# Meta tokens in front of the second block's input tiles, four panels in two pieces of 264 columns

## The chip, the cores and the metric

The kernel runs on one core of one Trainium2 chip. The metric is the device time of one execution in microseconds (us): 1583.48 us, the median of 3 runs (1582.49 to 1584.28).

## The reference

Two transformer blocks, one after the other, on 512 tokens of width 1024. The part that the change touches is the entry of the second block. It puts 16 learned meta tokens in front of the 512 tokens, normalises every token by its root mean square, and projects all of them by one wide weight matrix:

```python
h = jnp.concatenate([jnp.zeros((b, PAD, d)), meta, x], axis=1)
hn = rms_norm_2(h, attn_norm_g[l])
proj = hn @ w_in[l]
aq, ak, av, bq, bkv, iq, ik, iw, gates = jnp.split(proj, IN_SPLITS_2, axis=-1)
```

Only the keys and values need the meta tokens: `ak` and `av` (keys and values of the sliding-window attention, which has sinks), `bkv` (the latent keys and values of the sparse attention) and `ik` (the keys of the indexer that chooses, for each query, the 128 rows that the sparse attention may see). `ik` goes through a layer norm, `bkv` through a root-mean-square norm. Queries and gates are needed for the 512 tokens alone.

## The kernel before, in words

Activations lie transposed in SBUF: features on the partitions, tokens along the row, so that a token tile is 128 x 512. Every float32 factor is split into a high and a low part (`xh`, `xl` for an input, `wh`, `wl` for a weight), and a product is three matmuls: high by high, high by low, low by high (`mm3`, line 654). A weight "panel" is 128 x 1024, eight pieces (k = 0 to 7) of 128 x 128; `dense` (line 659) runs a panel as 8 x 3 matmuls of 512 columns into one PSUM tile (`psd`; `pso` for the panel `2ik`). SyncE's queue loads a panel as `wr`, ScalarE casts it to `wh`, and in the second block's attention GpSimd makes the difference `wl` for every panel of 1024 columns (elsewhere VectorE does some or all).

The first block ends with a feed-forward stage, `ffn1` (line 1574). Its last eight panels (`fb0_3` to `fb7_3`) finish the tokens x[0] to x[7]; for each, `x_steps` (line 1644) makes the next input pair `xh`, `xl` (x times a gain, not yet times the norm) and adds squares for two norms. From these come R1 (the final norm of the first block) and then Rt (`R`, the second block's norm). The norm factor R is multiplied in when a panel's result is taken out of PSUM, so the panels `2iq0`, `2iq1`, `2ik`, `2ak`, `2av`, `2aq0` can start before R is known; `2bkv` comes some 100 us later, after eight gate panels.

The meta tokens go beside this. `meta_prep` (line 1750), called at the start of the second block's attention, loads them as a 128 x 8 x 16 tile, multiplies by the gain, splits them (`mh`, `ml`), squares them, and gets their norm by eight tiny float32 matmuls into a column `rm` of 16 rows. In the four panels with `meta=True`, `dense` issues three more matmuls for each k, with the 16 meta columns as weights and the panel's piece as the moving side (128 columns; 68 in `2ik`), into a PSUM tile `pss`. That result lies the other way round (tokens on the partitions). For `2ak` and `2bkv`, `meta_cols` (line 1860) scales it on VectorE (`mT`), turns it on TensorE, and copies it to the front of a 528-column tile; for `2av` it is scaled and split as it lies; for `2ik` it goes into the fifth part of the layer norm's tile.

The order of the work. All engines run their instructions in program order, and the program order comes from a planner in the kernel. `charge` (line 344) gives each instruction a cost: a matmul that is not plain float32 costs 0.42e-3 us per column, but at least 0.107. A panel's matmuls are emitted as they come; everything else is a chain of steps (`chain`, line 392), and a step is emitted as soon as the planned time of TensorE has passed the step's planned start (`pick`, line 413: earliest start first, then priority, then age). A step with a transpose thereby gets a fixed place between two k's of some panel. The planner knows nothing of one engine holding up another's memory access.

After `2aq0` the stage of the indexer and of the sliding-window attention begins (scores, softmax, transposes; VectorE also picks the top 128 of each row in rounds of 8).

Buffers: tiles `u` (34 slots), `v` (10 in the second block's attention, 42 in both feed-forward stages, `nvf`), and PSUM tiles `psd` 3, `pss` 2, `pst` 2, `pso` 1.

Of the kernel before, what the change touches and what calls it, by code (L numbers as in the profile page):

```python
# [8 lines left out]
F32 = mybir.dt.float32  # L9
F32R = mybir.dt.float32r  # L10
BF16 = mybir.dt.bfloat16
AF = mybir.ActivationFunctionType
OP = mybir.AluOpType
# [4 lines left out]
P = 128  # L18
T = 512
# [4 lines left out]
TK = T + NMETA  # L24
NEG = -1e30
# [227 lines left out]
class Prog:  # L253
    nu, nv1, nv2, nvf, nk = 34, 25, 10, 42, 7
# [404 lines left out]
    def dense(self, name, X, nk, evac, M=P, sub=1, meta=False, steps=1, tag="d"):  # L659

        whl = None
        for j in range(sub):
            if whl is None:
                whl = self.w_get(name)
            wh, wl = whl
            ps = self.ps(tag, steps)
            pm = self.ps("s") if meta else None
            for k in range(nk):
                x = X[k] if not callable(X) else X(k)
                if len(x) > 2:  # L670
                    self.ensure(x[2])
                o = (j * nk + k) * M
                a, b = wh[:, o:o + M], wl[:, o:o + M]
                self.mm3(ps[0:M], a, b, x[0], x[1], k == 0, k == nk - 1)
                if meta:
                    self.mm3(pm[0:NMETA, 0:M], self.mh[:, k], self.ml[:, k], a, b, k == 0, k == nk - 1)
                yield
            if meta:
                evac(j, ps, pm)
            else:  # L680
                evac(j, ps)
# [163 lines left out]
    def v_tile(self, label, ps, put):  # L845

        nc = self.nc
        st = {}

        def s1():  # L850
            st["t"] = self.scaled(ps)

        def s2():
            pt = self.ps("t", 2)
            for b in range(4):
                nc.tensor.transpose(pt[:, P * b:P * b + P], st["t"][:, P * b:P * b + P], self.ident)
            st["pt"] = pt[:].rearrange("p (b c) -> p b c", b=4)

        def s3():
            st["v"] = [self.v(F32R, (P, 4, P), name="vt") for _ in range(2)]  # L860
            for hh, vt in enumerate(st["v"]):
                self.hi(vt[:, :, 0:64], st["pt"][:, :, 64 * hh:64 * hh + 64])

        def s4():
            for hh, vt in enumerate(st["v"]):
                self.lo(vt[:, :, 64:128], st["pt"][:, :, 64 * hh:64 * hh + 64], vt[:, :, 0:64])
            put(st["v"])
        self.chain(label, s1, s2, s3, s4, after=("R",))
# [507 lines left out]
    def block1_attention(self):  # L1376
        nc, tc = self.nc, self.tc
        mm = nc.tensor.matmul
        with ExitStack() as c1:
# [11 lines left out]
            v1 = self.apool.tile([8, 640], F32, name="v1")  # L1391
            va, v2 = (self.apool.tile([P, PTW], F32, name="row", tag="pt%d" % x, bufs=1) for x in range(2))
            oh = []
# [250 lines left out]
    def x_steps(self, X, m, src, g, sts, pool):  # L1644

        hi, lo = pool(F32R, name="xh"), pool(F32R, name="xl")
        X[m] = (hi, lo)
        a, b = self.xg((hi, lo), src, g)

        def sq():  # L1650
            for n, scale in sts:
                self.sq_chain(n, m, src, scale)
        return [a, b, sq]
# [39 lines left out]
    def block1(self):  # L1693
# [4 lines left out]
        with ExitStack() as c:  # L1698
# [13 lines left out]
            X2 = {}  # L1712
            gg = self.v(shape=(P, 8), name="gg")
# [5 lines left out]
            def norms():  # L1719

                N["R1"] = self.rkeep.tile([P, T], F32, name="R1", tag="R", bufs=2)
                N["R"] = self.rkeep.tile([P, T], F32, name="Rt", tag="R", bufs=2)
                self.norm("R1", 0, x2, lambda: N["R1"][:])
                self.norm("pb", 1, x2, None, evac=lambda ps: nc.scalar.copy(N["R"], ps))
                self.chain("Rt", s2, *self.rstd_steps(lambda: st["t"][:], T, D, out=lambda: N["R"][:]), s3,
                           after=("pb", "R1"))
# [9 lines left out]
            def resid(m):  # L1736
# [4 lines left out]
                                                [(0, None), (1, self.pv("g_final", m))], self.u), norms)  # L1741
# [5 lines left out]
            self.X = lambda k: (self.ensure(("x", k)), X2[k])[1]  # L1747


    def meta_prep(self):  # L1750

        nc = self.nc
        mt = self.v(shape=(P, 8, NMETA))
        nc.sync.dma_start(mt, self.I["metaT"])
        self.mh = self.mpool.tile([P, 8, NMETA], F32R, name="mh")
        self.ml = self.mpool.tile([P, 8, NMETA], F32R, name="ml")
        t = self.v(shape=(P, 8, NMETA))
        self.rm = self.mpool.tile([P, 1], F32, name="rm")
        st = {}

        def s0():
            nc.vector.tensor_tensor(t, mt, self.pv("g2", 0, 8).unsqueeze(2).to_broadcast([P, 8, NMETA]), op=OP.mult)

        def s0a():
            self.hi(self.mh[:], t[:])
            nc.scalar.activation(mt, mt, AF.Square)

        def s0b():
            self.lo(self.ml[:], t[:], self.mh[:])

        def s1():
            st["ps"] = ps = self.ps("t")
            for k in range(8):
                nc.tensor.matmul(ps[0:NMETA, 0:2], mt[:, k], self.ones[:, 0:2], start=(k == 0), stop=(k == 7))
        self.chain("meta", s0, s0a, s0b, s1,
                   *self.rstd_steps(lambda: st["ps"][0:NMETA, 0:1], 1, D, rows=NMETA,
                                    out=lambda: self.rm[0:NMETA], tmp=lambda: self.small([P, 1])), at=8.0)

    def mT(self):
        return self.mpool.tile([P, P], F32, name=self.nm("mT"), tag="mT", bufs=2)  # L1780

    def idx_k(self):
        def ev(j, ps, pm):
# [3 lines left out]
            def s1():  # L1787
                st["t"] = self.scaled(ps, rows=68)
                k = st["k"] = self.tmp()
                k3 = st["k3"] = k[:, 0:320].rearrange("p (b c) -> p b c", b=5)  # L1790
                nc.gpsimd.memset(k3[:, 4], 0.0)
                nc.vector.tensor_scalar_mul(k3[0:NMETA, 4], pm[0:NMETA, 0:64], self.rm[0:NMETA])

            def s2():
                pt = self.ps("t")
                for b in range(4):
                    nc.tensor.transpose(pt[:, 68 * b:68 * b + 68], st["t"][0:68, P * b:P * b + P],
                                        self.ident[0:68, 0:68])
                st["z"] = pt[:, 0:272].rearrange("p (b c) -> p b c", b=4)

            def s3():
                k3, z = st["k3"], st["z"]
                nc.vector.tensor_copy(k3[:, 0:4], z[:, :, 0:64])
                nc.vector.tensor_scalar_mul(self.iw, z[:, :, 64:68], 0.0625)
# [4 lines left out]
                q = self.tmp()  # L1809
                q3 = q[:, 0:320].rearrange("p (b c) -> p b c", b=5)  # L1810
# [29 lines left out]
        yield from self.dense("2ik", self.X, KD, ev, M=68, meta=True, tag="o")  # L1840
# [19 lines left out]
    def meta_cols(self, st, ps, pm):  # L1860

        nc = self.nc

        def s1():
            f = st["f"] = self.kk()
            nc.vector.tensor_mul(f[:, NMETA:TK], ps, self.R)
            t = st["mt"] = self.mT()
            nc.vector.tensor_scalar_mul(t[0:NMETA], pm[0:NMETA, 0:P], self.rm[0:NMETA])

        def s2():  # L1870
            pt = st["pt"] = self.ps("t")
            nc.tensor.transpose(pt[:, 0:NMETA], st["mt"][0:NMETA], self.ident[0:NMETA, 0:NMETA])

        def s3():
            nc.vector.tensor_copy(st["f"][:, 0:NMETA], st["pt"][:, 0:NMETA])
        return [s1, s2, s3]

    def a_k(self):
        def ev(j, ps, pm):
            st = {}  # L1880

            def s4():
                for g in range(2):
                    self.stack_k("ak", st["f"], 64 * g, self.ak)
            self.chain("ak", *self.meta_cols(st, ps, pm), s4, after=("R", "meta"))
        yield from self.dense("2ak", self.X, KD, ev, meta=True)

    def a_v(self):
        def ev(j, ps, pm):
            nc = self.nc  # L1890
            self.v_tile("av", ps, self.av.extend)

            def s1():
                t = self.mT()
                nc.vector.tensor_scalar_mul(t[0:NMETA], pm[0:NMETA, 0:P], self.rm[0:NMETA])
                src = t[0:NMETA].rearrange("p (g d) -> p g d", g=2)
                self.split((self.avm[0:NMETA, :, 0:64], self.avm[0:NMETA, :, 64:128]), src)
            self.chain("av", s1, after=("meta",))
        yield from self.dense("2av", self.X, KD, ev, meta=True)

    def b_kv(self):
        def ev(j, ps, pm):
# [33 lines left out]
            self.chain("bkv", *self.meta_cols(st, ps, pm), s4, s5,  # L1936
# [3 lines left out]
        yield from self.dense("2bkv", self.X, KD, ev, meta=True)  # L1940
# [352 lines left out]
    def block2_attention(self):  # L2293
        nc, tc = self.nc, self.tc
        with ExitStack() as c:
# [21 lines left out]
            self.meta_prep()  # L2317
# [272 lines left out]
```

## Time and profile before

| | |
|---|---|
| median of 3 runs | 1583.48 us |
| the profiled execution | 1585.77 us, of which its span (first to last instruction) is 1584.0 us |
| TensorE busy | 1529.1 us, 97% of the span |
| VectorE busy | 914.6 us, 58% |
| ScalarE busy | 774.5 us, 49% |
| GpSimd busy | 251.7 us, 16% |
| granted clock of TensorE, mean | 0.984 of full speed |

In the profile a tile is named without its buffer number: `psd<-xh,wh` is a matmul into a `psd` tile with `xh` moving and `wh` as weights. PE is TensorE, PEld its weight loads, DVE VectorE, ACT ScalarE, POOL GpSimd. A matmul's duration includes its latency, so what a matmul costs in a stream is read from the distance between starts. A float32 matmul is recorded twice. All instructions are recorded by one helper (line 241), so groups are told apart by tiles and not by lines. `mk` is the top-k mask, `qs` the split queries, `kk` a 528-column tile, `cst` the identity for transposes, `Rt` the second block's norm.

### The profile page before, as it was taken

The page shows a single profiled execution, that of the slowest core. Times are in us where ns is not written, and L with a number is a line of the kernel's source. Part 1 is how long each engine was busy: PE and PEld are TensorE (multiplying, and loading weights), DVE is VectorE, ACT ScalarE, POOL GpSimd, SP SyncE. Part 2 cuts the span into 40 slices and gives each one's busy share as a digit, 9 for nine tenths or more (in the row PEclk, how much of TensorE's full clock was granted, in tenths as well). Part 3 has the DMA queues.
Part 4 walks back from the last instruction along what each step waited for, and adds up shares of the span by engine and source line. Part 5 has one row for each costly group of instructions (what it writes and reads, how often), then busy time and mean ns, then how long its engine had stood idle before and what let it go on. Part 6 is the DMA issues. An engine that isn't in the chain of part 4 may idle for free.

```text
span 1584.0 us, 19921 instructions
## 1 busy us (share of the span) xinstructions
PE 1529.1 (97%) x7400; PEld 1254.1 (79%) x7400; DVE 914.6 (58%) x1781; ACT 774.5 (49%) x1468; POOL 251.7 (16%) x176
## 2 busy tenths in 40 slices
PE   7999999999999999999998899899899999999997
PEld 3788888878888888888876787678688888888887
DVE  5587677762654243454576999666566432446445
ACT  5676687985343231323443784577544222332333
POOL 3344211102210000000233133321142000000001
PEclk9999999999999999999999999999999999999999
DMA  4444421113423333233323222231042233333411
GB/s 154 131 134 135 120 67 54 60 54 96 157 86 101 94 94 106 93 93 98 102 89 99 67 77 86 63 119 34 28 146 93 94 95 104 94 91 111 134 50 54
DMA packets 50257, 148.82 MB, mean 94 GB/s; under 512 B 6620, under 2 KB 10332, under 8 KB 50160
## 3 DMA queue, kind: packets, MB, share of 16 engines
q1 hardware_dynamic: 44352, 138.63, 28.0%
q0 software_dynamic: 3360, 4.46, 1.4%
q10 hardware_dynamic: 2448, 4.46, 0.8%
q8 instruction: 58, 0.95, 0.2%
q14 instruction: 39, 0.32, 0.1%
HBM read 138.11 MB, written 4.41 MB: 90 GB/s over the span
## 4 chain that ended last, share of the span: by engine, by line
PE 88%; DVE 7%; ACT 2%; DMA 1%; issue 1%; SPq 0%; POOL 0%; DVEq 0%; ACTq 0%; POOLq 0%
PE psd L241 75%; PE pss L241 5%; PE pso L241 4%; PE pst L241 4%; DVE tmp L241 1%; DVE sct L241 1%; DVE sm L241 1%; DVE qs L241 1%; DMA x<-xT 1%; ACT tmp L241 1%; DVE pt L241 0%; DVE P L241 0%; SPq L241 0%; DMA cscr<-c 0%; DVE ol L241 0%
## 5 line engine op out<-in xcount | busy, mean ns | idle before, releaser
L241 PE MATMUL psd<-xh,wh 128*128 128x512 f32 (+1 forms) x1128 | 453.8, 402 | 8.5 <-ACT xh L241 8.5
L241 PE MATMUL psd<-xh,wl 128*128 128x512 f32 (+1 forms) x1128 | 443.6, 393 | 1.6 <-DVE wl L241 1.6
L241 PE MATMUL psd<-xl,wh 128*128 128x512 f32 (+1 forms) x1128 | 443.5, 393 | 0.3 <-DVE xl L241 0.2
L241 ACT CAST wh<-wr 128x1024 fp32r<-128x1024 f32 (+1 forms) x232 | 242.1, 1044 | 350.1 <-PE psd L241 195.0
L241 POOL TENSOR_TENSOR wl<-wr,wh 128x1024 fp32r<-128x1024 f32 x72 | 178.3, 2478 | 531.3 <-ACT wh L241 511.4
L241 PEld LDWEIGHTS psd<-xh,wh 128*128 128x128 f32 (+1 forms) x1128 | 213.5, 189 | 52.6 <-ACT xh L241 9.8
L241 DVE TENSOR_TENSOR wl<-wr,wh 128x1024 fp32r<-128x1024 f32 (+1 forms) x160 | 195.9, 1225 | 99.2 <-ACT wh L241 97.0
L241 PEld LDWEIGHTS psd<-xh,wl 128*128 128x128 f32 (+1 forms) x1128 | 212.9, 189 | 48.6 <-DVE wl L241 2.0
L241 PEld LDWEIGHTS psd<-xl,wh 128*128 128x128 f32 (+1 forms) x1128 | 213.4, 189 | 43.9 <-issue 2.4
L241 ACT ACTIVATE P<-P,sm 128x256 f32<-128x256 f32 (+7 forms) x319 | 165.8, 545 | 27.7 <-DVE sm L241 27.2
L241 POOL TENSOR_TENSOR sq<-sq,tmp 128x512 f32<-128x512 f32 (+1 forms) x32 | 39.5, 1242 | 737.3 <-ACT tmp L241 730.9
L241 PE MATMUL psd<-hh,wl 128*128 128x512 f32 x384 | 149.4, 389 | 0.0
L241 PE MATMUL psd<-hl,wh 128*128 128x512 f32 x384 | 149.4, 389 | 0.0
L241 PE MATMUL psd<-hh,wh 128*128 128x512 f32 x384 | 149.4, 389 | 0.0
L241 PEld LDWEIGHTS psd<-hh,wl 128*128 128x128 f32 x384 | 72.1, 188 | 15.0
L241 PEld LDWEIGHTS psd<-hl,wh 128*128 128x128 f32 x384 | 72.1, 188 | 15.0
L241 PEld LDWEIGHTS psd<-hh,wh 128*128 128x128 f32 x384 | 72.1, 188 | 15.0
L241 DVE TENSOR_TENSOR pt<-pst,pt 128x384 fp32r<-128x384 f32 (+3 forms) x144 | 69.3, 498 | 16.5 <-ACT pt L241 15.7
L241 ACT ACTIVATE tmp<-psd 128x512 f32<-128x512 f32 x32 | 19.1, 597 | 106.8 <-PE psd L241 106.7
L241 DVE TENSOR_TENSOR tmp<-tmp 128x512 f32<-128x512 f32 (+1 forms) x33 | 22.7, 686 | 83.4 <-ACT tmp L241 83.4
L241 ACT CAST pt<-pst 128x384 fp32r<-128x384 f32 (+3 forms) x144 | 58.4, 439 | 16.5 <-PE pst L241 15.2
L241 PE MATMUL pst<-cst,P 128*128 128x128 f32 (+1 forms) x416 | 63.1, 280 | 2.7 <-DVE pt L241 2.7
(368 smaller groups left out, 2276.8 us busy)
## 6 DMA issues: line engine op xcount, KB each, us to landing
wr<-wall SPq DMA_DIRECT2D x231, 512.0 KB, 3.5
wr<-wall SPq DMA_DIRECT2D x8, 384.0 KB, 3.6
kk<-v2scr SPq DMA_DIRECT2D x8, 264.0 KB, 4.5
x<-xT SPq DMA_DIRECT2D x8, 256.0 KB, 8.3
wb<-v1scr SPq DMA_DIRECT2D x8, 256.0 KB, 3.8
xr<-xT ACTq DMA_DIRECT2D x8, 256.0 KB, 4.4
xscr<-xr SPq DMA_DIRECT2D x8, 256.0 KB, 2.0
x<-xscr ACTq DMA_DIRECT2D x8, 256.0 KB, 4.8
```

The source lines that it names most:

```text
L241: return f(*a, **k)
```

## The change

The second block's input pairs become 128 x 528, with the 16 meta columns in front (gain multiplied in, split); the other panels read columns 16 to 527. `meta_prep` moves to the start of `ffn1`'s last eight panels: the load of the meta tokens, their gain, their squares and the eight matmuls for their norm (now with the 128 x 128 tile of ones as weights and 16 moving columns, so that the norm comes out along a row, on all partitions) are issued there, and the norm is written to the front of the 528-column `Rf`. A new chain `("xm", m)` for each of the eight input tiles casts 16 columns on ScalarE and makes the difference on GpSimd.

A new `dense_meta` replaces `dense(meta=True)` for `2ik`, `2ak`, `2av`, `2bkv`: for each k, six matmuls of 264 columns, into two PSUM tiles (one of the panel's own kind, one `pss`). `scaled_meta` takes the result out in two VectorE multiplies of 248 and 264 columns and one of 16, or two of 264. With that `2ak` and `2bkv` lose the scaling, the turn and the copy for meta; `2av` and `2ik` get a turn of 16 columns more.

Besides, `nvf` goes from 42 to 41 (a small tile `gg` leaves that pool), an 8 x 640 tile `v1` early in the first block becomes a slice of a larger one, and the layer norm of `ik` uses one temporary less.

```diff
-    nu, nv1, nv2, nvf, nk = 34, 25, 10, 42, 7
+    nu, nv1, nv2, nvf, nk = 34, 25, 10, 41, 7
...
-                if meta:
-                    self.mm3(pm[0:NMETA, 0:M], self.mh[:, k], self.ml[:, k], a, b, k == 0, k == nk - 1)
...
+    def dense_meta(self, name, evac, M=P, tag="d"):
+
+        wh, wl = self.w_get(name)
+        ps = self.ps(tag), self.ps("s")
+        for k in range(KD):
+            self.X(k)
+            xh, xl = self.XM[k]
+            a, b = wh[:, k * M:k * M + M], wl[:, k * M:k * M + M]
+            for n, (w, x) in enumerate(((a, xh), (a, xl), (b, xh))):
+                for e in range(2):
+                    self.mms(ps[e][0:M, 0:HT], w, x[:, HT * e:HT * e + HT], k == 0 and n == 0, k == KD - 1 and n == 2)
+            yield
+        evac(ps)
+
+    def scaled_meta(self, dst, ps, rows=P, M=NMETA):
+
+        nc = self.nc
+        R, w = self.Rf, HT - M
+        nc.vector.tensor_mul(dst[0:rows, 0:w], ps[0][0:rows, M:HT], R[0:rows, M:HT])
+        nc.vector.tensor_mul(dst[0:rows, w:w + HT], ps[1][0:rows, 0:HT], R[0:rows, HT:TK])
+        if M:
+            m = self.small([P, M])
+            nc.vector.tensor_mul(m[0:rows], ps[0][0:rows, 0:M], R[0:rows, 0:M])
+            return m
...
     def meta_prep(self, R):
...
+                nc.tensor.matmul(ps[:, 0:NMETA], self.ones, mt[:, k], start=(k == 0), stop=(k == 7))
+        self.chain("mt", s0, at=4.0)
+        self.chain("meta", s1, *self.rstd_steps(lambda: st["ps"][:, 0:NMETA], NMETA, D, out=lambda: R[:, 0:NMETA],
+                                                tmp=lambda: self.small([P, NMETA])), after=("mt",))
...
-    def meta_cols(self, st, ps, pm):
+    def meta_cols(self, st, ps):
...
         def s1():
-            f = st["f"] = self.kk()
-            nc.vector.tensor_mul(f[:, NMETA:TK], ps, self.R)
-            t = st["mt"] = self.mT()
-            nc.vector.tensor_scalar_mul(t[0:NMETA], pm[0:NMETA, 0:P], self.rm[0:NMETA])
-
-        def s2():
-            pt = st["pt"] = self.ps("t")
-            nc.tensor.transpose(pt[:, 0:NMETA], st["mt"][0:NMETA], self.ident[0:NMETA, 0:NMETA])
-
-        def s3():
-            nc.vector.tensor_copy(st["f"][:, 0:NMETA], st["pt"][:, 0:NMETA])
-        return [s1, s2, s3]
+            st["f"] = self.kk()
+            self.scaled_meta(st["f"], ps, M=0)
+        return [s1]
...
-            self.meta_prep()
```

## Rows read from the trace of the kernel before

**Rows 1.** The page's chain that ended last, by engine

```profile
PE 88%; DVE 7%; ACT 2%; DMA 1%; issue 1%; SPq 0%; POOL 0%; DVEq 0%; ACTq 0%; POOLq 0%
```

**Rows 2.** Waits of PE, 800 to 1170 us: us in total, times, longest

```profile
PE pst L241 <- DVE tmp L241: 8.7, 2, 5.3
PE pss L241 <- DVE sm L241: 6.1, 4, 3.9
PE pst L241 <- DVE kk L241: 2.4, 1, 2.4
```

**Rows 3.** Windows: length, busy PE, PEld, DVE, ACT, POOL; clock; DMA share; GB/s

```profile
840.00:860.00 20.00, 20.00 (x111) 15.36 (x109) 8.36 (x21) 5.13 (x10) 7.87 (x8) 0.91 0.52 128
...
880.00:900.00 20.00, 15.78 (x84) 13.73 (x85) 17.35 (x52) 12.96 (x38) 2.40 (x1) 0.83 0.28 84
...
1000.00:1020.00 20.00, 16.73 (x66) 13.72 (x67) 10.64 (x16) 10.00 (x15) 4.34 (x2) 0.83 0.09 27
```

**Rows 4.** Timeline of PE in 2ik and 2ak: start us, us, instruction

```profile
824.55 0.43 PE L241 MATMUL pso<-xh,wh 128*68 128x512 f32 x1
...
829.50 0.47 PE L241 MATMUL psd<-xh,wh 128*128 128x512 f32 x1
...
844.44 0.44 PE L241 MATMUL psd<-xh,wh 128*128 128x512 f32 x1
...
845.18 0.22 PE L241 MATMUL pss<-wh,mh 128*16 128x128 f32 x1
...
845.36 0.45 PE L241 MATMUL psd<-xh,wh 128*128 128x512 f32 x1
```

**Rows 5.** Timeline of PE: matmuls of 272 and of 256 columns

```profile
863.46 0.41 PE L241 MATMUL pss<-kk,qs 128*128 128x272 f32 x2
863.71 0.40 PE L241 MATMUL psd<-xh,wh 128*128 128x512 f32 x1
...
1540.15 0.28 PE L241 MATMUL psd<-hl,wk 128*128 128x256 f32 x1
...
1540.51 0.28 PE L241 MATMUL psd<-hl,wk 128*128 128x256 f32 x1
```

**Rows 6.** Groups by form, PEld: the weight loads of these 256-column matmuls (busy us, mean ns)

```profile
L241 PEld LDWEIGHTS psd<-hh,wk 128*128 128x128 f32 x192 | 30.1, 192 | 0.1
```

**Rows 7.** Timeline of PE at the meta norm in 2ik

```profile
822.38 0.20 PE L241 MATMUL pss<-wl,mh 128*16 128x68 f32 x1
823.08 0.20 PE L241 MATMUL pss<-wh,ml 128*16 128x68 f32 x1 [0.50 <-DVE ml L241]
...
823.69 0.45 PE L241 MATMUL pso<-xh,wh 128*68 128x512 f32 x1
```

**Rows 8.** Timeline of PEld, then of PE: a 16-column float32 matmul with the ones

```profile
975.28 0.19 PEld L241 LDWEIGHTS pst<-kk,ones 128*128 128x128 f32 x1 [0.24 <-issue]
...
975.42 0.48 PE L241 MATMUL psd<-xh,wh 128*128 128x512 f32 x1
```

**Rows 9.** Timeline and window (busy PE, clock) of PE around the long wait

```profile
837.77 0.71 PE L241 MATMUL pst<-cst,tmp 68*128 68x68 f32 x4 [5.29 <-DVE tmp L241]
...
838.23:843.39 5.16, 5.16 (x21) 0.50 0.75 242
```

**Rows 10.** Timeline of DVE from the norm to 2ik's scaling

```profile
818.67 2.48 DVE L241 TENSOR_TENSOR v<-v,pvt 128x128 f32<-128x128 f32 x1
...
829.50 1.27 DVE L241 SCALAR_TENSOR_TENSOR tmp<-psd,Rt 128x512 f32<-128x512 f32 x2
...
832.13 4.87 DVE L241 TENSOR_TENSOR qs<-tmp,qs 64x512 fp32r<-64x512 f32 x4
837.02 0.69 DVE L241 TENSOR_TENSOR tmp<-pso,Rt 68x512 f32<-68x512 f32 x1
```

**Rows 11.** Timeline of POOL in the same stretch

```profile
818.47 2.53 POOL L241 TENSOR_TENSOR wl<-wr,wh 128x1024 fp32r<-128x1024 f32 x1 [6.21 <-ACT wh L241]
...
833.91 2.54 POOL L241 TENSOR_TENSOR wl<-wr,wh 128x1024 fp32r<-128x1024 f32 x1 [5.87 <-ACT wh L241]
```

More of the change, by code (lines that the diff above doesn't have):

```diff
@@ L24 @@
 TK = T + NMETA
+HT = TK // 2
 NEG = -1e30
@@ L657, in mm3, with dense @@
         self.mms(ps, al, bh, False, stop)
-    def dense(self, name, X, nk, evac, M=P, sub=1, meta=False, steps=1, tag="d"):
+    def dense(self, name, X, nk, evac, M=P, sub=1, steps=1, tag="d"):
         whl = None
@@ L666, in dense @@
             ps = self.ps(tag, steps)
-            pm = self.ps("s") if meta else None
             for k in range(nk):
@@ L674, in dense @@
                 self.mm3(ps[0:M], a, b, x[0], x[1], k == 0, k == nk - 1)
-                if meta:
-                    self.mm3(pm[0:NMETA, 0:M], self.mh[:, k], self.ml[:, k], a, b, k == 0, k == nk - 1)
                 yield
[L678 to L681, printed above, removed]
+            evac(j, ps)
+    def dense_meta(self, name, evac, M=P, tag="d"):
[19 more added lines that the diff above has]
+            return m
     def rstd_steps(self, ps, w, n, rows=P, out=None, tmp=None):
@@ L843, in c_rows, with v_tile @@
         self.chain(label, lambda: self.dma(t[64:68], self.cscr[h, r:r + 4]), after=("fl",))
-    def v_tile(self, label, ps, put):
+    def v_tile(self, label, ps, put, meta=None):
         nc = self.nc
@@ L850, in s1 @@
         def s1():
-            st["t"] = self.scaled(ps)
+            if meta is None:
+                st["t"] = self.scaled(ps)
+            else:
+                st["t"] = self.tmp()
+                st["m"] = self.scaled_meta(st["t"], ps)
         def s2():
@@ L867, in s4, with m1, m2 @@
             put(st["v"])
-        self.chain(label, s1, s2, s3, s4, after=("R",))
+        def m1():
+            st["pm"] = self.ps("t")
+            nc.tensor.transpose(st["pm"][0:NMETA, 0:P], st["m"], self.ident)
+        def m2():
+            src = st["pm"][0:NMETA, 0:P].rearrange("p (g d) -> p g d", g=2)
+            self.split((meta[0:NMETA, :, 0:64], meta[0:NMETA, :, 64:128]), src)
+        self.chain(label, s1, s2, s3, s4, *([] if meta is None else [m1, m2]),
+                   after=("R",) if meta is None else ("R", "meta"))
     def fox_proj(self, p):
@@ L1390, in block1_attention @@
                        at=18.0, prio=4)
-            v1 = self.apool.tile([8, 640], F32, name="v1")
             va, v2 = (self.apool.tile([P, PTW], F32, name="row", tag="pt%d" % x, bufs=1) for x in range(2))
+            v1 = va[0:8, W_ASC:W_ASC + 640]
             oh = []
@@ L1642, in w_out, with x_steps, c @@
         self.finish()
-    def x_steps(self, X, m, src, g, sts, pool):
-        hi, lo = pool(F32R, name="xh"), pool(F32R, name="xl")
+    def x_steps(self, X, m, src, g, sts, pool, meta=False):
+        if meta:
+            hi, lo = self.XM[m] = pool(F32R, (P, TK), name="xh"), pool(F32R, (P, TK), name="xl")
+            def c(hi=hi, lo=lo):
+                self.hi(hi[:, 0:NMETA], self.mt[:, m])
+                self.nc.gpsimd.tensor_sub(lo[:, 0:NMETA], self.mt[:, m], hi[:, 0:NMETA].bitcast(F32))
+            self.chain(("xm", m), c, after=("mt",), prio=3)
+            hi, lo = hi[:, NMETA:TK], lo[:, NMETA:TK]
+        else:
+            hi, lo = pool(F32R, name="xh"), pool(F32R, name="xl")
         X[m] = (hi, lo)
@@ L1711, in block1 @@
             self.w_out("wo", x, lambda m: self.x_steps(self.XD, m, x[m], self.pv("g_mlp", m), [(0, None)], self.v))
-            X2 = {}
-            gg = self.v(shape=(P, 8), name="gg")
+            X2, self.XM = {}, {}
+            gg = self.small([P, 8])
             nc.vector.tensor_mul(gg, self.pv("g_final", 0, 8), self.pv("g2", 0, 8))
@@ L1721, in norms @@
                 N["R1"] = self.rkeep.tile([P, T], F32, name="R1", tag="R", bufs=2)
-                N["R"] = self.rkeep.tile([P, T], F32, name="Rt", tag="R", bufs=2)
+                self.Rf = self.rkeep.tile([P, TK], F32, name="Rt", tag="R", bufs=2)
+                N["R"] = self.Rf[:, NMETA:TK]
+                self.meta_prep(self.Rf)
                 self.norm("R1", 0, x2, lambda: N["R1"][:])
@@ L1740, in block1 @@
             self.ffn1(x, lambda m: self.x_steps(X2, m, x[m], gg[:, m:m + 1],
-                                                [(0, None), (1, self.pv("g_final", m))], self.u), norms)
+                                                [(0, None), (1, self.pv("g_final", m))], self.u, True), norms)
             self.ensure(*x2)
@@ L1746, in block1, with meta_prep @@
                 self.chain("resid", lambda m=m: resid(m), after=("R1",), prio=7)
-            self.X = lambda k: (self.ensure(("x", k)), X2[k])[1]
-    def meta_prep(self):
+            self.X = lambda k: (self.ensure(("x", k), ("xm", k)), X2[k])[1]
+    def meta_prep(self, R):
         nc = self.nc
-        mt = self.v(shape=(P, 8, NMETA))
+        mt, self.mt = self.v(shape=(P, 8, NMETA), name="mt"), self.v(shape=(P, 8, NMETA), name="mt")
         nc.sync.dma_start(mt, self.I["metaT"])
[L1755 to L1758, printed above, removed]
         st = {}
         def s0():
-            nc.vector.tensor_tensor(t, mt, self.pv("g2", 0, 8).unsqueeze(2).to_broadcast([P, 8, NMETA]), op=OP.mult)
-        def s0a():
-            self.hi(self.mh[:], t[:])
+            nc.vector.tensor_tensor(self.mt, mt, self.pv("g2", 0, 8).unsqueeze(2).to_broadcast([P, 8, NMETA]),
+                                    op=OP.mult)
             nc.scalar.activation(mt, mt, AF.Square)
-        def s0b():
-            self.lo(self.ml[:], t[:], self.mh[:])
         def s1():
@@ L1773, in s1, with ev @@
             for k in range(8):
[L1774 to L1780, printed above, removed]
+                nc.tensor.matmul(ps[:, 0:NMETA], self.ones, mt[:, k], start=(k == 0), stop=(k == 7))
+        self.chain("mt", s0, at=4.0)
+        self.chain("meta", s1, *self.rstd_steps(lambda: st["ps"][:, 0:NMETA], NMETA, D, out=lambda: R[:, 0:NMETA],
+                                                tmp=lambda: self.small([P, NMETA])), after=("mt",))
     def idx_k(self):
-        def ev(j, ps, pm):
+        def ev(ps):
             nc = self.nc
@@ L1787, in s1 @@
             def s1():
-                st["t"] = self.scaled(ps, rows=68)
+                st["t"] = self.tmp()
+                st["m"] = self.scaled_meta(st["t"], ps, rows=68)
                 k = st["k"] = self.tmp()
@@ L1791, in s1 @@
                 nc.gpsimd.memset(k3[:, 4], 0.0)
-                nc.vector.tensor_scalar_mul(k3[0:NMETA, 4], pm[0:NMETA, 0:64], self.rm[0:NMETA])
             def s2():
@@ L1798, in s2 @@
                                         self.ident[0:68, 0:68])
+                nc.tensor.transpose(pt[0:NMETA, 272:336], st["m"][0:64], self.ident[0:64, 0:64])
+                st["zm"] = pt[0:NMETA, 272:336]
                 st["z"] = pt[:, 0:272].rearrange("p (b c) -> p b c", b=4)
@@ L1803, in s3 @@
                 nc.vector.tensor_copy(k3[:, 0:4], z[:, :, 0:64])
+                nc.vector.tensor_copy(k3[0:NMETA, 4], st["zm"])
                 nc.vector.tensor_scalar_mul(self.iw, z[:, :, 64:68], 0.0625)
@@ L1808, in s3 @@
                 nc.vector.tensor_tensor(k3, k3, s[:].unsqueeze(2).to_broadcast([P, 5, 64]), op=OP.subtract)
-                q = self.tmp()
-                q3 = q[:, 0:320].rearrange("p (b c) -> p b c", b=5)
+                q3 = st["t"][:, 0:320].rearrange("p (b c) -> p b c", b=5)
                 nc.vector.tensor_mul(q3, k3, k3)
@@ L1839, in ev @@
                        after=("R", "meta"))
-        yield from self.dense("2ik", self.X, KD, ev, M=68, meta=True, tag="o")
+        yield from self.dense_meta("2ik", ev, M=68, tag="o")
     def stack_k(self, label, f, b, dst):
@@ L1858, in stack_k, with ev @@
         self.chain(label, s1, s2)
-    def meta_cols(self, st, ps, pm):
-        nc = self.nc
+    def meta_cols(self, st, ps):
         def s1():
-            f = st["f"] = self.kk()
-            nc.vector.tensor_mul(f[:, NMETA:TK], ps, self.R)
-            t = st["mt"] = self.mT()
-            nc.vector.tensor_scalar_mul(t[0:NMETA], pm[0:NMETA, 0:P], self.rm[0:NMETA])
-        def s2():
-            pt = st["pt"] = self.ps("t")
-            nc.tensor.transpose(pt[:, 0:NMETA], st["mt"][0:NMETA], self.ident[0:NMETA, 0:NMETA])
-        def s3():
-            nc.vector.tensor_copy(st["f"][:, 0:NMETA], st["pt"][:, 0:NMETA])
-        return [s1, s2, s3]
+            st["f"] = self.kk()
+            self.scaled_meta(st["f"], ps, M=0)
+        return [s1]
     def a_k(self):
-        def ev(j, ps, pm):
+        def ev(ps):
             st = {}
@@ L1884, in s4, with ev @@
                     self.stack_k("ak", st["f"], 64 * g, self.ak)
-            self.chain("ak", *self.meta_cols(st, ps, pm), s4, after=("R", "meta"))
-        yield from self.dense("2ak", self.X, KD, ev, meta=True)
+            self.chain("ak", *self.meta_cols(st, ps), s4, after=("R", "meta"))
+        yield from self.dense_meta("2ak", ev)
     def a_v(self):
[L1889 to L1899, printed above, removed]
+        yield from self.dense_meta("2av", lambda ps: self.v_tile("av", ps, self.av.extend, meta=self.avm))
     def b_kv(self):
-        def ev(j, ps, pm):
+        def ev(ps):
             nc = self.nc
@@ L1935, in s8 @@
                 self.split((self.cm[0][0:NMETA], self.cm[1][0:NMETA]), st["p2"][0:NMETA, 0:P])
-            self.chain("bkv", *self.meta_cols(st, ps, pm), s4, s5,
+            self.chain("bkv", *self.meta_cols(st, ps), s4, s5,
                        *self.rstd_steps(lambda: rs["a"], T, P, out=lambda: st["r"][:, 0:T]),
@@ L1939, in ev @@
                        s6, s7, s8, after=("R", "meta"))
-        yield from self.dense("2bkv", self.X, KD, ev, meta=True)
+        yield from self.dense_meta("2bkv", ev)
     def b_q(self, k):
```

## The prediction, made before the changed kernel was run

> **What bounds the kernel now.** I read the page's chain first: 88% of it is TensorE [rows 1]. So an instruction taken off TensorE is worth its own distance to the next start, wherever TensorE does not wait anyway. Next the waits of TensorE from the second block's attention on: one of 5.3 us for a VectorE tile `tmp`, 6.1 us in four pieces in the indexer's stage (longest 3.9), one of 2.4 us for `kk` [rows 2]. Then the windows: in 840 to 860 us VectorE has 8.4 us of work and TensorE is never idle, but its clock is 0.91; in 880 to 900 and 1000 to 1020 us, behind the 3.9 and the 2.4 us waits, it is 0.83 [rows 3]. A wait therefore costs more than itself here: behind the 5.3 us wait 5.16 us ran at a granted clock of 0.50, that is 1.2 GHz, which lost 2.6 us more [rows 9]. So two things are to be priced: TensorE work in four panels, and the wait in front of `2ik`'s transposes, 5.3 + 2.6 = 7.9 us, that lies in the middle of them.
>
> **The panels.** One k of `2ak` takes 845.36 - 844.44 = 0.92 us, one of `2ik` (829.50 - 824.55)/6 = 0.825 us, both at full clock; the three meta matmuls start only 0.06 us apart, but the first 512-column matmul behind them follows late [rows 4]. The new form is six matmuls of 264 columns. No row has 264. Three matmuls of 256 columns with three different weight tiles take 1540.51 - 1540.15 = 0.36 us, 0.120 each; two of 272 take 863.71 - 863.46 = 0.25, 0.125 each [rows 5]. These bound it on both sides; I take 0.1225, so 0.735 per k. Three panels of 128 outputs save 3 x 8 x (0.92 - 0.735) = 4.4 us, `2ik` 8 x (0.825 - 0.735) = 0.7. Together **-5.1 us** (bounds -4.8 and -5.5 by 0.125 and 0.120).
>
> **The meta norm.** Today it lies within `2ik`: from 822.38 to 823.69 us, of which two small matmuls are 0.06; 1.25 us go (0.50 of it a wait for `ml`) [rows 7]. It comes back in `ffn1`'s last panels, a pure TensorE stretch, with a 128-column weight load instead of a 16-column one. The row for that is the 16-column matmul with the ones in `2bkv`: its two records take 975.42 - 975.28 = 0.14 us [rows 8], eight make 1.1. If each of the 16 records cost a whole 0.19 us load it would be 3.0, at the pace of today's eight (at most 823.69 - 823.08) 0.6. I take 1.1, nearest in kind: **-0.15 us**, bounds -0.65 and +1.75. Its VectorE, ScalarE and GpSimd steps, the gain, the 16 casts and differences of the `xm` chains and the metaT load lie beside 40 us of dense matmuls; their cover is those panels' own length, and without it some 4 us of small instructions would show. SyncE's load of the meta tokens moves past the weight loads there; it waits for a `v` slot that the previous panel frees, before the next weight load is issued, so I charge nothing (at worst one panel load later by a wait of under 1 us).
>
> **Turns and evacuation.** `2ak` and `2bkv` lose a 16-row turn each, `2av` and `2ik` gain one: -0.1 to +0.1, I take 0. On VectorE two multiplies of 264 columns stand for one of 512 (0.69 us for `tmp<-pso` [rows 10]); split in two they cost at most one more fixed part, and the scaling and copying of meta go. Nothing, within 0.3 us. `nvf` 41 for 42: at its fullest the feed-forward stage holds 16 input, 16 hidden, 8 accumulator tiles and one more, 41, and `gg` no longer holds a slot; nothing, and a slot that is late has two free PSUM tiles, two panels, as cover. The `v1` slice adds at most a wait in the first 45 us, off TensorE.
>
> **The long wait.** TensorE leaves `2ik` at 829.50 today, and waits until 837.77. The order on VectorE is: norm, the scaling of `2iq0` and `2iq1` (829.50 to 830.77), four `qs` differences (4.87 us), and only then `2ik`'s scaling at 837.02 [rows 10]. That order comes from the planner, which charges a k with meta 3 x 0.215 + 3 x 0.107 = 0.966 us and will charge 6 x 0.111 = 0.665. `2ik`'s end thereby moves forward by 2.4 us in its account, to about where the norm is planned to be ready, while the `qs` differences have to wait for ScalarE's casts in either case. So `2ik`'s multiplies should come straight behind those of `2iq0` and `2iq1`, ahead of the differences: ready near 831.3 (830.77, less some 0.5 us of meta work that leaves VectorE's queue, plus about 1 us). TensorE leaves `2ik` at 829.50 - 0.7 - 1.25 = 827.5 and finds the transposes two to four k's later, at 829.0 to 830.5. A wait of about 1.6 us is left. Behind it a second one becomes due: `2ik`'s layer norm, then five transposes. Its VectorE work now shares the queue with the `qs` differences, one of which is held up as before; I put 1.6 us there, and no half clock (the trace has it behind waits of 2.4 us and more [rows 2, 3]). So 7.9 - 3.2 = **-4.7 us**, bounds -7.9 (no wait left) and +2 (below).
>
> One VectorE entry goes that looks dear: the meta gain, 128 columns, 2.48 us [rows 10]. It ran while GpSimd made a `wl` from 818.47 to 821.00 [rows 11], and one of the four `qs` differences runs into the next `wl`. I count only some 0.3 us for it, since the next VectorE multiply would stand there instead. The Trainium skill (SBUF — State Buffer, "SBUF: two separate sides") states the same as a lock: of a VectorE instruction with two SBUF inputs and a GpSimd instruction, whichever starts first holds the shared port pair to its end. The trace agrees (2.48 us for a quarter of the columns of a 0.69 us row); without that rule the norm would come 2.2 us sooner and the sum would be -12.3.
>
> **Sum.** -5.1 - 0.15 + 0 - 4.7 = -10 us. The profiled execution took 1585.77 us, 2.3 above the median; it becomes 1575.8, and from the median 1583.48 the forecast is **1573.5 us**. Between `2aq0` and 945 us VectorE is busy for nine tenths and waits for what the panels deliver; it simply starts earlier, so I carry the gain through.
>
> **Rivals.**
> 1. *The order stays and VectorE decides.* If `2ik`'s scaling remains behind the differences, the transposes are ready at about 837.2 whenever TensorE comes, and the wait grows to 7.4 us. For it: VectorE runs later than the planner thinks, with no gap from the norm on. Against: the 2.4 us in the planner's account. Then only k's behind the wait count: -0.6, -5 x 0.185, -1.5 for `2av`, -1.5 for `2bkv`, +1.1 for the norm's matmuls in the dense stretch, which shift both engines: -3.4, less what a longer wait may add: 1580.5.
> 2. *Other waits go too.* `2bkv`'s chain has two steps fewer, so the 2.4 us wait for `kk` and the half clock behind it (0.83 over 20 us, 3.4 us lost) may go, and the 3.2 us that I left: -10 - 5.8 - 2 = 1565.5. For it: the chain lost a hop to TensorE and back. Against: what made `kk` late is VectorE's top-k rounds, which stay.
> 3. *Slower: new waits with half clock in the indexer's stage.* By `2av`'s end the planner thinks TensorE 3 x 2.4 = 7.2 us ahead of before, the chip gives 3.6 plus the wait. It then places scores and transposes earlier against a VectorE that is busy for 17.35 of 20 us [rows 3]. One more such wait costs as 880 to 900 us does, 3.9 + 3.4 = 7.3. From two on the gain is eaten: 1583.5 - 10 + 14.6 = 1588. Against: the stage's length is VectorE's work, which does not grow.
> 4. *Each piece pays its weight load.* If loads were not hidden, a piece would last its 192 ns [rows 6], 1.15 per k: 32 x 0.415 = 13.3 us more, less the first wait, which it would fill: 1585. Against: the rows of 256 columns, at 0.120 us with a 192 ns load each. The Trainium skill (TensorE: Matmul & The Clock Gate, "The mechanism") has this rule: a weight load overlaps with a running matmul only where the row groups differ. The trace disagrees, for these loads use all 128 rows and still hide.
>
> **How the numbers follow.** Forecast 0.60 (its own range 1569.5 to 1577.5), rival 2 0.16, rival 1 0.11, rival 3 0.08, rival 4 0.02, a gain of 3.2 to 6 us in between 0.03. What a measurement can tell from no change is 0.2%, 3.2 us. Faster: 0.60 + 0.16 + 0.03 = 0.79; within: rival 1 and half of rival 4, 0.12; slower 0.09. The range from 1564 to 1581 takes in rival 2 and rival 1 and leaves out rivals 3 and 4 and the tail below.
>
> **What would show it.** Right: six matmuls per k at 0.12 us in four panels; DVE `tmp<-pso` (in two pieces) directly behind the two `tmp<-psd,Rt`, ahead of `qs`; the wait in front of the 68-row transposes under 2.5 us and the clock at 1.00 between `2ak` and `2aq0`; no meta matmul in `2ik`. Wrong: pieces near 0.19 us; `qs` differences ahead of `2ik`'s scaling; a clock under 0.9 in a window of the indexer's stage that had 1.00; or new waits of TensorE in the feed-forward stages.

## The result: slower, and not where the change was made

The kernel after takes 1591.38 us (median of 4 runs, 1590.05 to 1592.05), the kernel before 1582.99 in the same comparison: ratio 1.0052, 95% interval 1.0039 to 1.0065. Forecast was 1573.5 us, range 1564 to 1581. The sign is wrong.

In the second block's attention the trace after looks much as forecast. Timeline of TensorE in `2ik` (start us, us, instruction):

```profile
833.89 0.28 PE L242 MATMUL pso<-xh,wh 128*68 128x264 f32 x1
834.01 0.28 PE L242 MATMUL pss<-xh,wh 128*68 128x264 f32 x1
834.13 0.28 PE L242 MATMUL pso<-xl,wh 128*68 128x264 f32 x1
...
834.61 0.28 PE L242 MATMUL pso<-xh,wh 128*68 128x264 f32 x1
```

Each 264-column matmul is a piece. A piece starts every 0.12 us, and a k takes 834.61 - 833.89 = 0.72 us, where one of `2ik` took 0.825 and one of `2ak` 0.92 [rows 4]. VectorE has the forecast order (timeline of DVE): the scaling of `2ik`, in pieces, stands directly behind that of `2iq0` and `2iq1`, ahead of the `qs` differences that preceded it [rows 10].

```profile
841.03 1.28 DVE L242 SCALAR_TENSOR_TENSOR tmp<-psd,Rt 128x512 f32<-128x512 f32 x2
842.23 0.41 DVE L242 TENSOR_TENSOR tmp<-pso,Rt 68x248 f32<-68x248 f32 x1
842.55 0.42 DVE L242 TENSOR_TENSOR tmp<-pss,Rt 68x264 f32<-68x264 f32 x1
842.89 0.17 DVE L242 TENSOR_TENSOR sm<-pso,Rt 68x16 f32<-68x16 f32 x1
843.09 1.39 DVE L242 TENSOR_TENSOR qs<-tmp,qs 64x512 fp32r<-64x512 f32 x2
```

So the 68-row transposes, which stood behind 5.29 us of waiting [rows 9], wait for nothing (timeline of PE; brackets would give the idle time before an instruction). The next three turns do wait, 1.32 + 2.43 + 0.38 = 4.1 us:

```profile
842.69 0.74 PE L242 MATMUL pst<-cst,tmp 68*128 68x68 f32 x4
...
855.97 0.89 PE L242 MATMUL pst<-cst,tmp 128*128 128x128 f32 x4 [1.32 <-DVE tmp L242]
859.98 1.19 PE L242 MATMUL pst<-cst,tmp 128*64 128x128 f32 x5 [2.43 <-DVE tmp L242]
861.55 0.38 PE L242 MATMUL pst<-cst,sm 128*16 128x128 f32 x1 [0.38 <-DVE kk L242]
```

Over the whole attention TensorE waits less. Waits of PE from 800 to 1170 us after (total, times, longest), against [rows 2]; all lines of that view sum to 27.4 us before and 18.8 after:

```profile
PE pst L242 <- DVE tmp L242: 7.1, 3, 3.4
...
PE pst L242 <- DVE kk L242: 1.4, 2, 1.1
PE pss L242 <- DVE sm L242: 1.3, 2, 0.9
```

Windows of after (length, busy PE and matmuls, granted clock, DMA share, GB/s), against [rows 3]. The half clock of 880 to 900 us is gone. The one behind the long wait [rows 9] has come again behind the new waits, where the clock is 0.54. The one of 1000 to 1020 us is still there, only earlier, from 997.7 us on, so that this window holds just a part of it.

```profile
857.20:864.00 6.80, 3.99 (x14) 0.54 0.15 28
...
880.00:900.00 20.00, 18.38 (x114) 1.00 0.29 93
1000.00:1020.00 20.00, 20.00 (x79) 0.89 0.16 51
```

In sum this is gain; the loss must be elsewhere. The page's chain, the first view that I read of before [rows 1], does not find it either: the one of after breaks off early (its shares sum to 44%).

```profile
PE 39%; DVE 4%; ACT 1%; issue 0%; DVEq 0%; ACTq 0%
```

The views that show it are the windows of the two feed-forward stages, which the change does not touch: TensorE is busy throughout at clock 1.00 in both kernels, and does fewer matmuls. First before, then after:

```profile
500.00:700.00 200.00, 200.00 (x884) 1.00 0.31 98
1300.00:1500.00 200.00, 200.00 (x884) 1.00 0.34 107
```

```profile
500.00:700.00 200.00, 200.00 (x863) 1.00 0.29 93
1300.00:1500.00 200.00, 200.00 (x863) 1.00 0.31 102
```

884 / 863 is 2.4% more time per matmul. The timeline of PE has it row by row. Before, ten steps take 642.09 - 639.82 = 2.27 us, 0.227 each:

```profile
639.82 0.39 PE L241 MATMUL psd<-xh,wl 128*128 128x512 f32 x1
640.05 0.39 PE L241 MATMUL psd<-xh,wh 128*128 128x512 f32 x1
...
642.09 0.39 PE L241 MATMUL psd<-xh,wh 128*128 128x512 f32 x1
```

After, 642.11 - 639.79 = 2.32 us, 0.232 each, for the same instructions on tiles of the same size:

```profile
639.79 0.39 PE L242 MATMUL psd<-xh,wh 128*128 128x512 f32 x1
640.02 0.39 PE L242 MATMUL psd<-xl,wh 128*128 128x512 f32 x1
...
642.11 0.39 PE L242 MATMUL psd<-xl,wh 128*128 128x512 f32 x1
```

I summed this over the neighbouring pairs of 512-column matmuls into `psd` and `pso` tiles that start at full clock and at most 0.28 us apart (5,109 before, 5,048 after). Their start-to-start times exceed 0.2267 us by 3.9 us in total before and by 26.9 us after: 23.0 us lost.

### The profile page after: what moved, and what is told of

Its sections match the earlier page's. It is cut to its first block, busy times and chain, and to the rows that moved or that the text cites. A ratio compares the mean times of both kernels' runs of the same rounds, so it can differ in the third digit from the quotient of the medians.

```text
span 1590.3 us, 19932 instructions
## 1 busy us (share of the span) xinstructions
PE 1544.0 (97%) x7400; PEld 1256.8 (79%) x7400; DVE 913.9 (57%) x1781; ACT 774.6 (49%) x1475; POOL 253.4 (16%) x184
## 5 line engine op out<-in xcount | busy, mean ns | idle before, releaser
L242 PE MATMUL psd<-xh,wh 128*128 128x512 f32 (+2 forms) x1128 | 455.1, 403 | 8.7 <-ACT xh L242 8.7
L242 PE MATMUL psd<-xh,wl 128*128 128x512 f32 (+2 forms) x1128 | 445.7, 395 | 1.6 <-DVE wl L242 1.6
L242 PE MATMUL psd<-xl,wh 128*128 128x512 f32 (+2 forms) x1128 | 446.5, 396 | 0.3 <-DVE xl L242 0.3
L242 PEld LDWEIGHTS psd<-hl,wh 128*128 128x128 f32 x384 | 72.3, 188 | 16.8
L242 PEld LDWEIGHTS psd<-hh,wl 128*128 128x128 f32 x384 | 72.3, 188 | 16.8
```

What stands on the lines that cost most here:

```text
L242: return f(*a, **k)
```

## The experiments

The instructions of those stages are the same in both kernels; the addresses of their tiles are not. Tiles stand in SBUF in the order constants, R (2), raw weights `wr`, `wh`, `wl`, `tmp`, `u`, `v`. Before, `wr` begins at byte 27136 of a partition, `u` at 72192 with slots of 2048 bytes, `v` at 141824: all multiples of 256. After, R slots are 64 bytes wider and some small constants went; `wr` (and with it `wh`, `wl`, `tmp`) begins at 27008, 128 past a multiple of 256, `v` at 143872, a multiple of it, and the `u` slots of 2112 bytes lie at every multiple of 64. The feed-forward stages stream `v` tiles against `wh` and `wl`. By "distance" I mean the start of the streamed tile less that of the weight tile, modulo 256 unless said otherwise. A run named `b_` is an edit of the kernel before, `a_` one of the kernel after.

**The unused 128 bytes, in three places.** In the kernel before, ahead of the weight pool (`b_gap_w`) or ahead of the `u` pool (`b_gap_u`); in the kernel after, ahead of the weight pool (`a_gap_w`):

```
+        self.gap = ctx.enter_context(tc.tile_pool(name="gap", bufs=1)).tile([P, 32], F32, name="gap")
         self.wpool = ctx.enter_context(tc.tile_pool(name="w", bufs=1))      # b_gap_w, a_gap_w
         self.upool = ctx.enter_context(tc.tile_pool(name="u", bufs=1))      # b_gap_u: ahead of this line
```

> The kernel before with one unused tile of 128 bytes per partition between the tile of R and the weight tiles, so that weight tiles, tmp and everything behind them start 128 bytes later (all of them started at a multiple of 512 bytes before). No instruction differs. Theory W (what the change costs is where the weight tiles start: after the change they start 384 bytes past a multiple of 512, and a 512-column matmul of the dense stages then takes 0.232 instead of 0.2267 us): step 0.232 us in the two FFN stages, time near 1583 + 17 = 1600 us. Theory M (it is the start of the moving tiles): the same 1600 us, told apart by the next kernel. Theory N (not the layout, but the new instructions or the new order): step 0.2267, time 1583 us.

Measured: 1582.03 us, ratio to before 0.9997 (0.9988 to 1.0007); 884 matmuls in 500 to 700 us. Theories W and M both expected 1600: a common shift costs nothing.

> The kernel before with the same unused 128 bytes placed behind weight tiles and tmp, so that only the moving tiles (u, v and what lies behind) start 128 bytes later, the weight tiles stay. Theory W: step 0.2267 us, 1583 us. Theory M: step 0.232 us, near 1600 us. Theory N: 1583 us.

Measured: 1609.27 us, ratio 1.0174 (1.0153 to 1.0195). Window 500 to 700 us, and a piece of the timeline of PE:

```profile
500.00:700.00 200.00, 200.00 (x859) 1.00 0.30 93
```

```profile
644.79 0.40 PE L241 MATMUL psd<-xh,wh 128*128 128x512 f32 x1
645.02 0.39 PE L241 MATMUL psd<-xl,wh 128*128 128x512 f32 x1
645.25 0.40 PE L241 MATMUL psd<-xh,wl 128*128 128x512 f32 x1
...
646.89 0.39 PE L241 MATMUL psd<-xh,wh 128*128 128x512 f32 x1
```

Not one instruction differs from the kernel before, and it is 27 us slower. Nine steps take 2.10 us, 0.233 each; in the nanoseconds of the records they are 229 and 237 or 238 in turn, which the rows' rounding blurs. That is a regular pattern, not a collision now and then.

> The kernel after with 128 unused bytes ahead of the weight tiles: these start again at a multiple of 512 bytes, the 2112-byte u slots and the v tiles stay at other offsets. Theory W: step back to 0.2267 us in the FFN stages, and the time falls from 1591 to near 1573 us, which is where the panels and the shorter wait alone would have put it. Theory M: step stays 0.232, time 1591 us or a little above. Theory N: no change, 1591 us.

Measured: 1591.79 us, ratio to before 1.0060 (1.0043 to 1.0077), as the kernel after. So W fell: weight tiles at a multiple of 512 bytes do not help, since `v` moved by the same 128. Together the three say that neither start counts, but the two against each other: 0 in `b_gap_w`, 128 in `b_gap_u`, after and `a_gap_w`. That became theory R.

**One edit that crosses the two.** G, a tile of 384 bytes among the constants, is allocated between `tmp` and `u` instead. In the kernel after (`a_G`) weights and `v` then have distance 0; in the kernel before (`b_G`) they lose it.

```
-        self.G = self.cpool.tile([P, 4, 24], F32, name="G")
+        self.G = ctx.enter_context(tc.tile_pool(name="g", bufs=1)).tile([P, 4, 24], F32, name="G")
         self.upool = ctx.enter_context(tc.tile_pool(name="u", bufs=1))
```

> The kernel after with one tile, G (384 bytes per partition, written once in block 1), allocated between tmp and the u tiles instead of ahead of R. No instruction differs. Weight tiles and v tiles then both start at multiples of 512 bytes, as they did before the change; the 2112-byte u slots stay scattered. Theory R (what counts is the distance of the moving tile from the weight tile modulo 512 bytes, zero before, 128 after): step 0.2267 us in both FFN stages, 0.231 where the moving tiles are u slots, time 1591.4 minus about 1600 + 1250 matmuls x 5.6 ns = 1574 to 1576 us. Theory S (some other effect of the change slows the FFN): step 0.232, time 1591 us.

Measured: 1574.21 us (6 runs, 1571.74 to 1577.67), ratio to before 0.9947 (0.9932 to 0.9963). The feed-forward stages have the pace of before; 380 to 480 us, where `u` tiles are streamed, has not (439 matmuls before, 431 after). Windows of `a_G`:

```profile
380.00:480.00 100.00, 100.00 (x432) 1.00 0.37 116
500.00:700.00 200.00, 200.00 (x884) 1.00 0.32 97
...
1300.00:1500.00 200.00, 200.00 (x884) 1.00 0.34 106
```

> The kernel before with the same edit: G allocated between tmp and u, so that weight tiles start 384 bytes earlier and u and v tiles stay. Distance of moving from weight tiles 384 modulo 512. Theory R: the step goes from 0.2267 to 0.232 or 0.233 us in all dense stages and the time from 1582.5 to 1600 to 1610 us. Theory S: 1582.5 us.

Measured: 1608.61 us, ratio 1.0158 (1.0143 to 1.0173), 859 matmuls in 500 to 700 us. The same edit takes 17 us from one kernel and gives 26 to the other, as R expected; S is out.

**Other distances.** 64 and 256 bytes ahead of the `u` pool in the kernel before. For 256 to fit, the 64 bytes of the gates' bias lie in the gap:

```
+        self.gap = ctx.enter_context(tc.tile_pool(name="gap", bufs=1)).tile([P, 16], F32, name="gap")   # b_gap_u64; 64 columns in b_gap_u256
         self.upool = ctx.enter_context(tc.tile_pool(name="u", bufs=1))
...
-            self.nbg = self.mpool.tile([P, 16], F32, name="nbg")       # b_gap_u256
+            self.nbg = self.gap[:, 0:16]
```

> The kernel before with 64 unused bytes between tmp and u: distance 64 instead of 128. If theory R's distance counts modulo 64, step 0.2267 us and 1582.5 us; if any distance that is no multiple of 128 (or of 512) costs, step 0.232 or more, 1600 to 1610 us.

Measured: 1592.43 us (2 runs), ratio 1.0060 (1.0042 to 1.0079). Mean step in the feed-forward stages 0.2289 us, between the two values (in the nanoseconds of the records 226, 229 and 232 in turn, one for each matmul of a triple); the window:

```profile
500.00:700.00 200.00, 200.00 (x876) 1.00 0.32 97
```

So 64 is neither free, nor as dear as 128: my expectation had named only these two.

> The kernel before with 256 bytes between tmp and u (the 64 bytes of the gates' bias are put in them, so that the rest fits). Distance 256: if the step depends on the distance modulo 256, 0.2267 us and 1582.5 us; if modulo 512, 0.229 to 0.234 us and 1592 to 1612 us. Distances 64, 128 and 384 gave 0.2289, 0.2333 (0.2324 in some stretches) and the same in the FFN stages.

Measured: 1580.67 us, ratio 0.9991 (0.9979 to 1.0002), 884 matmuls in 500 to 700 us. The period is 256 bytes, not 512 as I had put it for theory R.

**Which pair.** A gap inside the weight pool of the kernel before: ahead of `wl` (`wr` and `wh` stay, `wl` and all behind it move), or ahead of `wh` (only `wr` stays).

```
+                if not self.wsplit:
+                    self.gap = self.wpool.tile([P, 32], F32, name="gap", tag="gap", bufs=1)
                 hi = self.wpool.tile([P, 1024], F32R, name=self.nm("wh"), tag="wh", bufs=self.nwh)   # b_gap_wh
                 lo = self.wpool.tile([P, 1024], F32R, name=self.nm("wl"), tag="wl", bufs=self.nwh)   # b_gap_wl: ahead of this line
```

> The kernel before with 128 unused bytes between the tiles of wh and those of wl: wl, tmp, u and v move together, raw weights and wh stay. If the pair is the weight that TensorE loads and the tile that it streams, the matmuls with wh (two in three) are the misaligned ones, and the step lies between 0.2267 and 0.233 or at it, time 1590 to 1610 us. If it is tmp or the raw weights against the moving tiles, step 0.2267 us with wh and wl alike, 1582.5 us (tmp) or 0.233 (raw weights).

Measured: 1611.59 us (2 runs), ratio 1.0181 (1.0163 to 1.0200). `tmp` and `wl` kept their distance from the streamed tiles, so `tmp` is out. All three matmuls of a triple are slow, not only the two with `wh`; timeline of PE:

```profile
639.92 0.39 PE L241 MATMUL psd<-hh,wh 128*128 128x512 f32 x1
640.15 0.40 PE L241 MATMUL psd<-hl,wh 128*128 128x512 f32 x1
640.39 0.40 PE L241 MATMUL psd<-hh,wl 128*128 128x512 f32 x1
640.62 0.39 PE L241 MATMUL psd<-hh,wh 128*128 128x512 f32 x1
```

In nanoseconds the step behind a matmul with `wh` is 232 or 233 on average, and behind one with `wl`, which is itself at distance 0, it is 235. So the distance of a matmul's own pair does not decide its own step: theory R holds for the stream as a whole, when `wh` and `wl` both agree with the streamed tile, and not matmul by matmul.

> The kernel before with 128 unused bytes between the raw weight tiles and those of wh: the raw tiles (written by DMA, read by ScalarE, VectorE and GpSimd) stay, wh, wl, tmp, u and v move together. If what counts is the distance of the tiles that TensorE streams from the tiles that it loads as weights, step 0.2267 us and 1582.5 us. If it is the raw tiles' distance from the rest, step 0.233 us and about 1610 us.

Measured: 1582.72 us, ratio 1.0003 (0.9988 to 1.0018), so the raw tiles are out. What is left are the tiles that TensorE loads as weights and those that it streams. The runs, by distance in the feed-forward stages (the ratios of the kernels after, `a_gap_w` and `a_G` hold what the change gains as well):

| kernel | distance, bytes | matmuls in 500 to 700 us | ratio to before |
|---|---|---|---|
| before, `b_gap_w`, `b_gap_wh` | 0 | 884 | 1, 0.9997, 1.0003 |
| `b_gap_u256` | 256, that is 0 | 884 | 0.9991 |
| `a_G` | 0 (`u` scattered) | 884 | 0.9947 |
| `b_gap_u64` | 64 | 876 | 1.0060 |
| after, `a_gap_w` | 128 | 863 | 1.0052, 1.0060 |
| `b_gap_u`, `b_G` | 128 | 859 | 1.0174, 1.0158 |
| `b_gap_wl` | 128 for `wh`, 0 for `wl` | 859 | 1.0181 |

**Open.** That it is TensorE's own reading of the two that interferes is the likeliest, since the pattern is periodic in its steps and returns in both feed-forward stages, but this is argued and not shown: VectorE, ScalarE and GpSimd write the same tiles, and no run separates that. Nor does a run say why a third of the matmuls at distance 0 is not faster in `b_gap_wl`. Why distance 128 gives 863 in one layout and 859 in another is open too. A layout that also puts the `u` tiles at distance 0 was not tried: slots widened to a multiple of 256 bytes (2304) would take 34 x 192 = 6,528 bytes more of each partition, where even the 256 of `b_gap_u256` fitted only with the gates' bias put into them.

## Why the prediction was wrong

**The step that failed** is one that the prediction priced at nothing: widening R and the `u` slots by 64 bytes. Under "Turns and evacuation" it counted slots (`nvf` 41 for 42) and asked whether one would be late; that every tile behind a widened one starts elsewhere, and that a matmul's pace depends on it, had no term, no bound and no rival. All bounds were on the work near the change, so the range could not reach 1591. By the runs this term is 1591.38 - 1574.21 = 17.2 us for weights against `v`; by the sums of excess 26.9 - 10.1 = 16.8. The scattered `u` slots cost a further 10.1 - 3.9 = 6.2 us, which `a_G` still pays.

The other terms, by the traces:

- *Panels, -5.1.* With 0.72 to 0.73 us per k (0.735 forecast) it is 24 x 0.195 + 8 x 0.10 = 5.5 us saved: right. (The stated bounds are slightly off: 0.125 and 0.120 us per piece give -4.7 and -5.6, not -4.8 and -5.5.) Rival 4 is out: a piece takes 0.12 us.
- *Meta norm, -0.15.* The sixteen records go from 778.5 to 780.1 us, with the last one 1.7 us in place of the 1.25 that went: +0.45, inside its bounds; the price from the pair in `2bkv` was 0.6 too low. The group of the view by tile, after:

```profile
L242 PE MATMUL pst<-mt,ones x16: 178/263/263, 778.5 to 780.1; 128*128 128x16 f32 x16
```

- *Long wait, -4.7.* Half right. The planner's order turned as argued, so rival 1 is out, and the wait in front of the 68-row transposes went altogether (1.6 us were to stay). But 4.1 us of new waits came behind it (1.6 forecast), and the half clock that I ruled out came with them: 3.99 us of work at 0.54, some 1.8 us. Of 7.9 us about 2 were gained here. The reason given for no half clock, that the trace has it behind waits of 2.4 us and more, read too few rows: before, TensorE ran at 0.50 from 1045.0 to 1048.4 us too, behind waits of 0.70 and 1.15 us (at 1043.14 and 1044.73).
- *Other waits.* Held at no gain, and there the kernel gained most. All waits of the attention sum to 20.5 us in `a_G` against 27.4; without the long wait and the 0.5 us for `ml` before, both counted above, and the three new waits after (4.1 us in `a_G` too), that is 16.4 against 21.6. TensorE also worked less at half clock, 13.8 us against 22.1 us, which is 4.1 us less lost, 3.4 of them away from the long wait. This part is uncertain, since each kernel has one trace: the stretches at half clock make 27 us before, but 20 us in `b_gap_w`, which has the same instructions, and 17 in `a_G`. Rival 2 had the kind of gain, but only part of the place: the waits for `kk` shrank from 2.4 to 1.4 us and the half clock behind them from 6.8 to 3.4 us, while the 3.9 us wait for `sm`, with the half clock of 880 to 900 us behind it, went unnamed by any rival as a gain. Windows at half clock, before and then `a_G`:

```profile
836.80:843.60 6.80, 5.83 (x23) 4.40 (x24) 4.95 (x15) 0.42 (x2) 0.00 (x0) 0.50 0.59 192
884.60:891.40 6.80, 5.36 (x26) 5.29 (x27) 4.43 (x19) 4.36 (x14) 0.00 (x0) 0.50 0.37 111
1000.60:1007.40 6.80, 4.13 (x11) 3.26 (x12) 4.41 (x9) 3.96 (x7) 0.00 (x0) 0.50 0.00 0
1045.00:1048.40 3.40, 3.40 (x14) 2.65 (x12) 3.30 (x7) 1.72 (x5) 2.44 (x1) 0.50 0.00 0
1133.80:1137.20 3.40, 3.33 (x8) 2.42 (x9) 0.68 (x1) 0.02 (x1) 0.00 (x0) 0.50 0.00 0
```

```profile
846.10:852.90 6.80, 4.33 (x13) 3.15 (x14) 4.41 (x10) 0.79 (x2) 1.95 (x3) 0.50 0.10 20
986.10:989.50 3.40, 2.64 (x7) 2.17 (x8) 3.37 (x8) 2.71 (x6) 0.00 (x0) 0.50 0.00 0
1033.90:1037.30 3.40, 3.40 (x11) 2.25 (x10) 1.36 (x7) 1.96 (x7) 0.00 (x0) 0.50 0.49 137
1129.40:1132.80 3.40, 3.40 (x10) 2.62 (x9) 1.91 (x3) 0.62 (x1) 0.00 (x0) 0.50 0.34 134
```

Waits of PE in `a_G`, against [rows 2]:

```profile
PE pst L242 <- DVE tmp L242: 7.2, 3, 3.4
PE pss L242 <- DVE sm L242: 3.1, 4, 1.6
...
PE pst L242 <- DVE kk L242: 1.4, 2, 1.0
```

So the local gain was not 10 us, but near 1582.99 - 1574.21 + 6.2 = 15, an estimate. The traces bear it out: from the first matmul of `2ik` to the last one that streams `oh`, near the end of the attention, `a_G`, the kernel after and `a_gap_w` take 326.6 to 327.8 us, and the kernel before, `b_gap_w`, `b_gap_wh` and `b_gap_u256` 340.7 to 342.8. That `a_G` lands on 1574.2, next to the forecast 1573.5, is in part chance: 5 us of gain that the forecast did not have against 6.2 us that the `u` slots still cost. Two of the prediction's smaller sums slip by 0.1 to 0.2 us (-10 - 2.2 is -12.2, and rival 2's -17.8 gives 1565.7); nothing rests on them. Rival 3, the one slower case, had another mechanism (waits with half clock in the indexer's stage); the trace shows fewer of these, not more. The last sentence of "What would show it" named the feed-forward stages, but for waits of TensorE: there are none, it is its pace that fell.

## What to carry to other kernels

A change of a tile's size moves every tile behind it. Before pricing such a change at nothing, work out the starts of the tiles that TensorE loads and streams, before and after, modulo 256 bytes; if they drift apart, pad until they agree again. And where a change makes a kernel slower although its own stage got faster, compare the count of matmuls in a busy window of a stage that it does not touch.

## What the runs showed of the hardware

- A stream of 128x128 by 128x512 float32r matmuls, each with its own weight load, starts one every 0.2267 us on average where streamed and weight tiles have the same start modulo 256 bytes (`before`, `b_gap_u256`, `a_G`), every 0.2289 at distance 64 (`b_gap_u64`), every 0.232 to 0.233 at 128 (after, `b_gap_u`).
- The Trainium skill (TensorE: Matmul & The Clock Gate, "Step-by-step: what each phase is for") says that loading the next tile's weights does not take SBUF bandwidth from the running matmul, because TensorE has two independent read ports. The runs here put a limit to reading it as independence: with instructions unchanged, the place of the two operands against each other changes the pace by up to 2.9% (884 / 859). Whether it is those two reads that interfere is not shown.
- Shorter matmuls at mixed distances did not show it. The last stage of the kernel after streams `v` tiles in 256 columns against weights that lie in scattered `u` slots, and nine steps take 1550.91 - 1549.84 = 1.07 us, 0.119 each; 0.120 before [rows 5]. Timeline of PE (x2 is two matmuls):

```profile
1549.84 0.29 PE L242 MATMUL psd<-hl,wk 128*128 128x256 f32 x1
1549.97 0.40 PE L242 MATMUL psd<-hh,wk 128*128 128x256 f32 x2
...
1550.91 0.28 PE L242 MATMUL psd<-hl,wk 128*128 128x256 f32 x1
```
